# Hybrid decoder layer: small steps of the first two pairs moved, head norms over two tiles, and the softmax heads of the gate pair begun two groups later

## The chip, the cores and the metric

The kernel runs on one core of a Trainium2 chip. The metric is the device time of one execution in microseconds (us); the median of several runs is compared. The core's engines are named as in the profile: PE is TensorE (matmuls), PEld its weight loads, DVE is VectorE, ACT is ScalarE, POOL is GpSimd, and SP is SyncE, whose queue here issues nearly every transfer, one after the other.

## The reference

One decoder layer on 512 positions of width 2048, all in float32. Cut to what matters here:

```python
h = rms_norm(x, norm1_g)
proj = h @ w_in
qa, ka, va, ra, ga, qb, kb, vb = split(proj)
log_g = log_sigmoid(ga @ gla_gate_w2 + gla_gate_b) / 16
out_a = gla_mixer(qa, ka, va, ra, log_g, gla_onorm_g)    # ends in rms_norm(o) * silu(ra)
qb, kb = rms_norm(qb, q_norm_g), rms_norm(kb, k_norm_g)  # per head of 128
out_b = dilated_mixer(qb, kb, vb, rel_bias)              # causal softmax heads with a bias
x = x + concatenate([out_a, out_b]) @ w_out
h2 = rms_norm(x, norm2_g)
x = x + (silu(h2 @ w_gate) * (h2 @ w_up)) @ w_down
```

`qa` and `ka` are 512 columns wide, `va` and `ra` 1024 each, `ga` 16, and `qb`, `kb`, `vb` 1024 each. `gla_mixer` is a gated linear attention of 4 heads over chunks of 64 positions. `dilated_mixer` has 8 heads of 128 columns; the kernel computes it as one causal softmax whose bias depends on the distance alone.

## The kernel before

**Pairs.** All large products go through one scheme. A pair computes two blocks of 512 output columns for all 512 rows by seven half-sized products (Strassen's, in Winograd's form) in place of eight: `P1`, `P5`, `P6`, `P3`, `P7`, `P2`, `P4` in the later pairs. In the pairs around the change each product sums over four contraction groups, which makes 28 items of 12 matmuls with 128x512 outputs. The 12 are for precision: the operand is kept as a rounded part and a remainder, and so is the weight. Eight matmuls take the weight's rounded part `wh`, four its remainder `wl`. ScalarE makes `wh` (L373; L519 in the first pair), VectorE makes `wl` (L377; L527) and the differences of weight blocks that some products need (L298; L514). Such an item is called a group below, and in the prediction.

**Ends of products.** Accumulators are few (four banks, `acc`, and four more, `bank`, for everything else). Where a product ends whose value is needed again, ScalarE copies it to a `seed` tile (L324 with the row scale; L542 in the first pair, without), from a pool of six. A later product's end adds its own accumulator to that tile (`close`). Then `final` takes the finished block of 256 rows by 512 columns as two tiles: `final_proj` stores it (L1065) to device memory, from where the heads load it.

**The first pair** gives `qa` and `ka` and has its order written by hand, in the string `PLAN`. `h.k` makes `wh` of item k and `l.k` its `wl`; `mH.k` and `mL.k` are its matmuls; `sq`, `nA`, `nB`, `nC` build the row norm of `x` (squares, then on `xms` the mean, L691, Ln and Exp, L694 and L695, and a Newton step; the digit is the half of the rows); `gh` and `rank` belong to the 16 columns `ga`; `seedX`, `closeX` and `sclX` copy, close and scale block X. `scla` scales block `a`, a part of `qa`, by the norm of half 0 (L550), after which `final` stores it.

**The later pairs** are written by `stream`. After the eighth matmul of each group it calls `step()`, which counts down what was put off with `later(n, fn)` and then takes as many steps of the generators in `background` as the pair's `rate` says: `rate((84, 0.5))` is one step in two groups. The generators are the gates (`gates`), the bias tables (`bias_tables`, fed by a one-hot table), the four heads of linear attention (`gla_head`) and four couples of softmax heads (`dil_heads`, eight steps of two heads). The second step of a couple transposes and scales `q` and `k` (L954, L955). Each later one makes, for one block of 128 rows, the scores with Exp (L969), reciprocal and scaling (L973), then their transposition (L980, copied by L983) and the product with the values (L987, L999). With `hold` set, as in the gate pair, a weight difference is placed behind the last score emitted.

**Order.** SP's queue follows the code as emitted; a scheduler sets the order on PE, ACT and DVE from it. Names such as `oT`, `PT`, `v`, `kT` are single tiles that all background work uses in turn: a new user waits for the last.

**The pairs around the change.** Pair 2 gives `va` and runs `gates`, `bias_tables` and the first linear heads: four gate matmuls (L795, from `gas`, L789) give `ls_d` (L802), a head loads its part of it as `T` (L822), cumulates it on TensorE (L833), transposes `q` and `k` (L849), scales `q` into `qT` (L857) and forms its scores (L873). Pairs 3 and 5 give `qb` and `kb`, normalised per head in `heads_norm`; pair 4 gives `vb`; pair 6, the gate pair, gives `ra`. Its `final_gate` loads the finished linear attention `og` (L1103), multiplies it by `ra` (L1119), forms the sigmoid by Exp, Ln and Exp (L1120 to L1122), multiplies again (L1123), and two groups later transposes the result (L1078) into the operand of the product with `w_out`; pieces of that operand are split as `GATE` and `OUT` list them. In the gate pair the last two couples of softmax heads run, at a `rate` of their own.

## Time and profile before

| | us |
|---|---|
| median of 3 runs (1940.41 to 1941.84) | 1941.62 |
| the profiled execution | 1938.88 |
| its span, first to last instruction | 1937.1 |
| TensorE busy | 1918.9 |
| VectorE busy | 1650.3 |
| ScalarE busy | 1094.8 |
| GpSimd busy | 16.8 |

The profile is of one execution. A page gives busy times, groups of instructions and a chain of waits; from the trace behind it come the list of waits by engine, windows and timelines. A row of waits has the engine and tile that waited, the engine and tile that ended the wait, and total us, number and longest. A timeline row has start and duration in us, the engine (SPq is SP issuing a transfer), line, operation, tiles, and in brackets how long the engine stood idle before it and what ended that. A row of windows has the stretch, its length, and for each engine its busy time and its instructions; where it is limited to one line, that line's alone. Its last three figures are TensorE's granted clock as a share of full speed, the share of the transfer engines in use, and GB/s. Engines work side by side, so a busy time adds to the span only where another engine waits for it.

### The profile page before, as it was taken

What the parts mean: (1) busy time and instruction counts of PE and PEld (TensorE: products, weight loads), DVE (VectorE), ACT (ScalarE), POOL (GpSimd) and SP (SyncE); (2) the same over time, 40 slices, a digit from 0 to 9 for tenths busy, and PEclk for the clock granted to TensorE, in tenths of its full rate; (3) what the DMA queues carried; (4) which work ended last, traced back from release to release, by engine and by line L of the source; (5) the groups of instructions that cost most, each with busy time, mean ns of one, the idle gap of its engine ahead of it and who ended that gap; (6) DMA issues with size and microseconds to landing.
All of it is one profiled execution on the core that took longest, in us unless ns stands there. A gap on an engine that the chain in (4) does not pass through costs nothing.

```text
span 1937.1 us, 25614 instructions
## 1 busy us (share of the span) xinstructions
PE 1918.9 (99%) x9178; PEld 1662.9 (86%) x9178; DVE 1650.3 (85%) x1936; ACT 1094.8 (57%) x1634; POOL 16.8 (1%) x25
## 2 busy tenths in 40 slices
PE   9999999999999999999999999999999999999999
PEld 7888888888888888888888888888888888888887
DVE  8896887778799999878878878878879989989987
ACT  9564564667766675544544545544546646546443
POOL 1000100000000000000000000000000000000000
PEclk9999999999999999999999999999999999999999
DMA  8536555444536564455454454453555865855762
GB/s 337 195 109 220 168 180 173 140 157 146 185 131 208 177 213 130 136 180 161 137 180 156 138 185 142 152 185 122 172 169 175 292 210 184 297 190 180 244 218 66
DMA packets 150360, 345.75 MB, mean 178 GB/s; under 512 B 15494, under 2 KB 42671, under 8 KB 150232
## 3 DMA queue, kind: packets, MB, share of 16 engines
q1 hardware_dynamic: 149944, 343.98, 52.9%
q8 instruction: 72, 1.18, 0.3%
q14 instruction: 56, 0.46, 0.1%
q10 hardware_dynamic: 288, 0.14, 0.0%
HBM read 286.10 MB, written 60.31 MB: 179 GB/s over the span
## 4 chain that ended last, share of the span: by engine, by line
PE 87%; DVE 6%; DMA 4%; issue 2%; ACT 1%; SPq 0%; POOL 0%; DVEq 0%; ACTq 0%; POOLq 0%
PE acc L402 79%; DVE wl L377 2%; PE acc L474 2%; PE bank L1078 1%; PE bank L987 1%; PE bank L963 1%; DVE wa L298 1%; PE bank L980 0%; DVE AS L199 0%; DMA T<-in_xt 0%; DMA k<-in_gw 0%; PE bank L760 0%; DMA wb<-in_w_in 0%; PE bank L954 0%; PE bank L474 0%
## 5 line engine op out<-in xcount | busy, mean ns | idle before, releaser
L402 PE MATMUL acc<-wh,AS 128*128 128x512 f32 x3008 | 711.8, 379 | 0.0
L402 PEld LDWEIGHTS acc<-wh,AS 128*128 128x128 f32 x3008 | 568.2, 189 | 81.2 <-ACT wh L373 0.5
L373 ACT CAST wh<-wa 128x1024 fp32r<-128x1024 f32 x376 | 394.3, 1049 | 396.3 <-PE acc L402 367.6
L402 PE MATMUL acc<-wh,AA 128*128 128x512 f32 x2256 | 534.7, 380 | 0.5 <-ACT wh L373 0.5
L377 DVE TENSOR_TENSOR wl<-wa,wh 128x1024 fp32r<-128x1024 f32 x376 | 456.7, 1217 | 73.0 <-ACT wh L373 47.3
L402 PEld LDWEIGHTS acc<-wh,AA 128*128 128x128 f32 x2256 | 427.1, 189 | 61.7 <-ACT wh L373 0.9
L402 PE MATMUL acc<-wl,AS 128*128 128x512 f32 x1504 | 393.8, 384 | 1.8 <-DVE wl L377 1.6
L402 PEld LDWEIGHTS acc<-wl,AS 128*128 128x128 f32 x1504 | 280.0, 189 | 51.4 <-DVE wl L377 10.2
L402 PE MATMUL acc<-wl,AA 128*128 128x512 f32 x1128 | 296.4, 385 | 0.2
L402 PEld LDWEIGHTS acc<-wl,AA 128*128 128x128 f32 x1128 | 209.9, 189 | 31.4 <-DVE wl L377 2.4
L373 ACT CAST wh<-wb 128x1024 fp32r<-128x1024 f32 x94 | 98.6, 1049 | 123.6 <-PE acc L402 118.9
L373 ACT CAST wh<-wc 128x1024 fp32r<-128x1024 f32 x94 | 98.5, 1048 | 115.9 <-PE acc L402 107.8
L373 ACT CAST wh<-wd 128x1024 fp32r<-128x1024 f32 x94 | 98.6, 1049 | 102.2 <-PE acc L402 98.6
L377 DVE TENSOR_TENSOR wl<-wc,wh 128x1024 fp32r<-128x1024 f32 x94 | 114.5, 1219 | 40.4 <-ACT wh L373 40.4
L377 DVE TENSOR_TENSOR wl<-wd,wh 128x1024 fp32r<-128x1024 f32 x94 | 114.4, 1219 | 36.5 <-ACT wh L373 29.6
L298 DVE TENSOR_TENSOR wa<-wc,wa 128x1024 f32<-128x1024 f32 x94 | 114.4, 1219 | 32.9 <-DMA wc<-in_w_gate 22.1
L377 DVE TENSOR_TENSOR wl<-wb,wh 128x1024 fp32r<-128x1024 f32 x94 | 114.0, 1216 | 5.0 <-ACT wh L373 4.8
L298 DVE TENSOR_TENSOR wa<-wb,wa 128x1024 f32<-128x1024 f32 x94 | 113.6, 1218 | 1.2 <-DMA wb<-in_w_in 0.5
L298 DVE TENSOR_TENSOR wb<-wd,wb 128x1024 f32<-128x1024 f32 x94 | 114.0, 1216 | 0.4
L298 DVE TENSOR_TENSOR wa<-wd,wa 128x1024 f32<-128x1024 f32 x94 | 112.9, 1215 | 0.1
L340 DVE SCALAR_TENSOR_TENSOR seed<-acc,rs,seed 128x512 f32<-128x512 f32 x96 | 70.4, 745 | 29.4 <-PE acc L402 29.3
L324 ACT ACTIVATE seed<-acc,rs 128x512 f32<-128x512 f32 x96 | 60.6, 682 | 5.0 <-PE acc L402 4.9
(320 smaller groups left out, 1315.5 us busy)
## 6 DMA issues: line engine op xcount, KB each, us to landing
wa<-in_w_gate SPq DMA_DIRECT2D x44, 512.0 KB, 3.5
wb<-in_w_up SPq DMA_DIRECT2D x44, 512.0 KB, 4.3
wd<-in_w_up SPq DMA_DIRECT2D x44, 512.0 KB, 4.3
wc<-in_w_gate SPq DMA_DIRECT2D x44, 512.0 KB, 3.5
wa<-in_w_in SPq DMA_DIRECT2D x24, 512.0 KB, 4.6
wc<-in_w_in SPq DMA_DIRECT2D x24, 512.0 KB, 3.5
wb<-in_w_in SPq DMA_DIRECT2D x24, 512.0 KB, 5.4
wd<-in_w_in SPq DMA_DIRECT2D x24, 512.0 KB, 4.4
```

The costliest lines, as they stand in the source:

```text
L298: nc.vector.tensor_tensor(src, other, src, op=ALU.subtract)
L324: nc.scalar.activation(halves(t), unfolded(src[m]), AF.Copy, scale=self.scale(half, m))
L340: nc.vector.scalar_tensor_tensor(halves(seed[m]), unfolded(src[m]), self.scale(half, m), halves(seed[m]), op0=ALU.mult, op1=ALU.add,)
L373: nc.scalar.copy(high[k], sources[k])
L377: nc.vector.tensor_tensor(low[k], sources.pop(k), high[k].bitcast(F32), op=ALU.subtract)
L402: nc.tensor.matmul(p.dst[prod][m], a[:, jj, hl, m * P : (m + 1) * P], folded(w[i][:, jj, :]), start=fresh and g == 0 and i == 0 and jj == ...
L474: recent["pe"] = nc.tensor.matmul(dst[name][m], a[:, jj, hl, m * P : (m + 1) * P], folded(w[:, jj, :]), start=(name, m) not in opened, sto ...
L963: nc.tensor.matmul(lp[:, :n], qh[:, b * P : (b + 1) * P], kh[:, :n], start=True, stop=True)
L987: nc.tensor.matmul(op, vh[:, k, :], lgs[b][:, k * P : (k + 1) * P], start=(k == 0), stop=(k == b))
L1078: nc.tensor.transpose(bk[:, jj, m * P : (m + 1) * P], tiles[m][:, f : f + P], ident)
```

## The change

Five edits of order and of small steps; no matmul is added or removed.

1. In `PLAN` the norm of row half 0 (`nA.0`, `nB.0`, `nC.0`) and the scaling of block `a` (`scla.0`, `scla.1`) move ahead, the scaling from behind `h.24` to right behind `h.19`; `gh.1` moves one item back.
2. `gates` gets a yield ahead of the copy of the gate columns and another ahead of its four matmuls, so these come later; the first part of the one-hot table in `bias_tables` uses tile `PT` in place of `v`.
3. `heads_norm` takes both tiles of a block at once: eight squares, then one chain of mean, Ln, Exp and Newton step over eight columns in place of two over four; the stores follow both. The small tile `rt` doubles for it.
4. `final_gate` has its `og` loaded two groups into the product that closes the block, by `ahead`, a hook that `begin` already had with three groups; it was loaded at the close.
5. The gate pair's `rate` holds the background back for four groups in place of three and for two in place of one, and then takes 0.93 steps a group in place of 0.9.

```diff
--- before.py
+++ after.py
@@ -71,29 +71,29 @@
 
 
 PLAN = """
...
-mL.18 mH.19 +W.20 nA.1 h.20 lo.S2.3 mL.19 lo.S3.3 h.21 mH.20 l.20 nB.1 l.21 mL.20 h.22 +S4.3
-mH.21 nC.1 l.22 mL.21 h.23 nA.0 mH.22 nB.0 l.23 nC.0 mL.22 h.24 mH.23 scla.0 l.24 scla.1 mL.23
...
+seedc.1 lo.S4.1 mL.14 hi.S4.2 l.15 h.16 mH.15 lo.S4.2 seedc.0 l.16 mL.15 nA.0 lo.A22.1 mH.16
+lo.A22.2 hi.S3.2 +W.17 mL.16 +W.19 h.17 nB.0 rank.1 lo.S3.0 lo.S3.2 hi.S3.1 +W.22 l.17 mH.17 +W.18
+D.d.3 D.b.3 lo.S3.1 nC.0 h.18 mL.17 +W.21 h.19 scla.0 scla.1 mH.18 l.18 hi.S3.3 l.19 mL.18 mH.19
...
 """
 
 
@@ -174,7 +174,7 @@
     ident, tri, stri, causal = (mats[:, i, :] for i in range(4))
 
     def rsqrt_mean(sq, n):
-        y = work("rt", (P, 4), bufs=4)[:, : sq.shape[-1]]
+        y = work("rt", (P, 8), bufs=4)[:, : sq.shape[-1]]
         nc.vector.tensor_scalar(sq, sq, 1.0 / n, EPS, op0=ALU.mult, op1=ALU.add)
         nc.scalar.activation(y, sq, AF.Ln)
         nc.scalar.activation(y, y, AF.Exp, scale=-0.5)
@@ -311,7 +311,7 @@
                 self.dst["P2"] = self.accs()
             ahead = getattr(self.final, "ahead", None)
             if ahead and prod in CLOSES:
-                later(3, lambda: ahead(*CLOSES[prod]))
+                later(getattr(self.final, "units", 3), lambda: ahead(*CLOSES[prod]))
 
         def seeds(self, src, half):
             res = []
@@ -657,7 +657,7 @@
         rel = work("T", (33, 8))
         nc.gpsimd.memset(rel[32:33, :], 1.0)
         load(rel[0:32, :], ins["rel_bias"])
-        for c0, cn, t0, t1 in ((0, 512, "v", "qT"), (512, NB - 512, "oT", "kT")):
+        for c0, cn, t0, t1 in ((0, 512, "PT", "qT"), (512, NB - 512, "oT", "kT")):
             oh = work(t0, (33, cn))
             load(oh, ins["onehot"][:, c0 : c0 + cn])
             bp = bank()
@@ -770,6 +770,7 @@
                          ap=[[0, 8], [512, 16], [1, 512]]))
         gbias = work("oT")
         load(gbias, bass.AP(tensor=ins["gla_gate_b"].tensor, offset=0, ap=[[0, P], [1, 512]]))
+        yield
         ga = work("k", (32, 512))
         nc.scalar.copy(ga, rank["p"][:32, :])
         ga4 = work("kT")
@@ -789,6 +790,7 @@
             nc.vector.tensor_tensor(
                 gas[r, :], ga4[r, :], gas[r, :].bitcast(F32), op=ALU.subtract
             )
+        yield
         yield
         for t in range(4):
             zp = bank()
@@ -1029,17 +1031,22 @@
             yield from g
 
 
-    def heads_norm(t):
-
-        ss = work("ss", (P, 4), bufs=4)
+    def heads_norm(tiles):
+
+        ss = work("ss", (P, 8), bufs=4)
         jk = work("jk", (P, P // 2)).bitcast(mybir.dt.bfloat16)
-        tv = t.rearrange("p (h d) -> p h d", h=4)
-        for h in range(4):
-            nc.scalar.activation(jk, tv[:, h, :], AF.Square, accum_out=ss[:, h : h + 1])
+        by_head = [t.rearrange("p (h d) -> p h d", h=4) for t in tiles]
+        for m in range(2):
+            for h in range(4):
+                nc.scalar.activation(
+                    jk, by_head[m][:, h, :], AF.Square, accum_out=ss[:, 4 * m + h : 4 * m + h + 1]
+                )
         rsqrt_mean(ss, P)
-        nc.vector.tensor_tensor(
-            tv, tv, ss.unsqueeze(2).to_broadcast([P, 4, P]), op=ALU.mult
-        )
+        for m in range(2):
+            nc.vector.tensor_tensor(
+                by_head[m], by_head[m],
+                ss[:, 4 * m : 4 * m + 4].unsqueeze(2).to_broadcast([P, 4, P]), op=ALU.mult,
+            )
 
     ready = {
         "va0": lambda: [gla_head(0), gla_head(1)],
@@ -1058,10 +1065,10 @@
                 tiles = emitted(acc_, lambda m: row_scale(half, m))
             name = (n1, n2)[which]
             dst = proj[name]
+            if name[:2] in ("qb", "kb"):
+                heads_norm(tiles)
             for m in range(2):
                 r = half * 256 + m * P
-                if name[:2] in ("qb", "kb"):
-                    heads_norm(tiles[m])
                 store(dst[r : r + P, :], tiles[m])
             if half == 1 and name in ready:
                 background.extend(ready[name]())
@@ -1095,13 +1102,16 @@
             store(dsts[b][half], d)
             done.add((id(dsts[b]), half))
 
+    normed = {}
+
+    def gate_ahead(half, which):
+        both = apool.tile([P, 2, 512], F32, name=nm("og"), tag="A")
+        for m in range(2):
+            load(both[:, m, :], ong_d[2 * half + m][:, which * 512 : (which + 1) * 512])
+        normed[half, which] = [both[:, m, :] for m in range(2)]
+
     def final_gate(half, which, tiles, acc_):
-        og = []
-        spare = apool.tile([P, 2, 512], F32, name=nm("og"), tag="A")
-        for m in range(2):
-            t = spare[:, m, :]
-            load(t, ong_d[2 * half + m][:, which * 512 : (which + 1) * 512])
-            og.append(t)
+        og = normed.pop((half, which))
         if tiles is None:
             tiles = [cpool.tile([P, 512], F32, name=nm("cr"), tag="C") for _ in range(2)]
             src = acc_
@@ -1133,6 +1143,8 @@
 
         later(2, turn)
 
+    final_gate.ahead, final_gate.units = gate_ahead, 2
+
     def part(src, half):
         def get(t=None):
             assert (id(src), half) in done
@@ -1235,7 +1247,7 @@
     pair(opx, rows_in, col(3072), col(4096), final_proj("qb0", "kb0"), flow, row_scale)
     pair(opx, rows_in, col(5632), col(5120), final_proj("vb1", "vb0"), flow, row_scale)
     pair(opx, rows_in, col(3584), col(4608), final_proj("qb1", "kb1"), flow, row_scale)
-    pair(opx, rows_in, col(2048), col(2560), final_gate, scripted(rate((3, 0), (1, 1), (1, 0), (1, 1), (1, 0.9)), GATE), row_scale, hold=True)
+    pair(opx, rows_in, col(2048), col(2560), final_gate, scripted(rate((4, 0), (1, 1), (2, 0), (1, 1), (1, 0.93)), GATE), row_scale, hold=True)
 
 
     rows_mix = [(1024 + 256 * g, 256 * order[g]) for g in range(4)]
```

The scheduler turns this into the following orders. A row gives the line, the operation, the tiles written and read, and the size; numbers in names count tiles.

ScalarE, at the end of the first pair, before: Ln and Exp of a row norm (L694, L695; the second such couple is half 0's), the casts of `wh` (L519), the scaling of block `a` (L550), and the next seeds (L542).

```order
L519 CAST wh_909<-wa_244 128x1024
L694 ACTIVATE rs_105<-xms 128x2
L695 ACTIVATE rs_105<-rs_105 128x2
L519 CAST wh_929<-wa_246 128x1024
L519 CAST wh_949<-wb_860 128x1024
L694 ACTIVATE rs_105<-xms 128x2
L695 ACTIVATE rs_105<-rs_105 128x2
L519 CAST wh_972<-wd_858 128x1024
L550 ACTIVATE seed_520<-seed_520,rs_102 128x512
L550 ACTIVATE seed_525<-seed_525,rs_102 128x512
L542 COPY seed_992<-acc_412 128x512
L542 COPY seed_994<-acc_413 128x512
```

The same place after the change, from the norm of half 0 to that of half 1 (L208 is an operand cast):

```order
L694 ACTIVATE rs_105<-xms 128x2
L695 ACTIVATE rs_105<-rs_105 128x2
L208 CAST AS_125_848<-xT_108 128x2x256
L519 CAST wh_870<-wb_264 128x1024
L519 CAST wh_877<-wb_271 128x1024
L550 ACTIVATE seed_520<-seed_520,rs_102 128x512
L550 ACTIVATE seed_525<-seed_525,rs_102 128x512
L208 CAST AS_132_893<-xT_114 128x2x256
L519 CAST wh_912<-wa_240 128x1024
L519 CAST wh_920<-wa_244 128x1024
L694 ACTIVATE rs_105<-xms 128x2
L695 ACTIVATE rs_105<-rs_105 128x2
```

The norm of half 0 stood behind six casts of `wh` that it now stands ahead of; the two scalings, which stood right ahead of the seeds, now have five casts of `wh` behind them before the seeds come.

TensorE, the first head of linear attention in pair 2, before: the last matmuls of pair 2 (L402), then the head's cumulation (L833, L834), transpositions (L849, `mats` holds the identity) and scores (L873), with nothing between.

```order
L402 MATMUL acc_1062<-wl_1679,AA_47_338 128x512
L402 MATMUL acc_1063<-wl_1679,AA_47_338 128x512
L833 MATMUL bank_1598<-mats,T_1553 128x128 x3
L834 MATMUL bank_1599<-T_1553,mats 128x512
L849 MATMUL bank_1652<-mats,q_1558 128x128 x4
L849 MATMUL bank_1653<-mats,k_1560 128x128 x4
L873 MATMUL bank_1691<-qT_1662,kT_1666 64x128
L873 MATMUL bank_1691<-L_1605,kT_1666 64x128
L873 MATMUL bank_1691<-qT_1662,kT_1666 64x128
```

The same head after the change (lines are two further on: L851 is the transposition, L875 the score):

```order
L851 MATMUL bank_1652<-mats,q_1558 128x128 x4
L851 MATMUL bank_1653<-mats,k_1560 128x128 x4
L402 MATMUL acc_1062<-wl_1621,AA_89_595 128x512
L402 MATMUL acc_1063<-wl_1621,AA_89_595 128x512
L402 MATMUL acc_1062<-wl_1621,AA_89_595 128x512
L402 MATMUL acc_1063<-wl_1621,AA_89_595 128x512
L402 MATMUL acc_1062<-wh_1636,AA_85_572 128x512 x2
L402 MATMUL acc_1063<-wh_1636,AA_85_572 128x512 x2
L402 MATMUL acc_1062<-wh_1636,AA_85_572 128x512 x2
L402 MATMUL acc_1063<-wh_1636,AA_85_572 128x512 x2
L875 MATMUL bank_1691<-qT_1662,kT_1666 64x128
L875 MATMUL bank_1691<-L_1605,kT_1666 64x128
```

Twelve matmuls now lie between the transpositions and the first score (eight rows, of which four stand for two matmuls each); the cumulation stands a group and a half further ahead, outside these rows.

ScalarE in the gate pair, where the second of its couples of softmax heads begins, before: scalings of `q` and `k` (L955), the first Exp of scores (L969), the six activations of the first gate close (L1120 to L1122).

```order
L955 ACTIVATE qT_4748<-bank_4788,gq 128x512
L955 ACTIVATE kT_4749<-bank_4794,gk 128x512
L198 CAST AA_941_4959<-top_4857 128x2x256
L373 CAST wh_4843<-wb_4346 128x1024
L969 ACTIVATE L_4824,mx_4825<-L_4824,mx_4825 128x128
L969 ACTIVATE PT_4833,mx_4834<-PT_4833,mx_4834 128x128
L373 CAST wh_4864<-wb_4383 128x1024
L373 CAST wh_4917<-wb_4404 128x1024
L983 COPY L_4824<-bank_4891 128x128
L983 COPY PT_4833<-bank_4902 128x128
L1120 ACTIVATE seed_4702<-seed_4702 128x512
L1120 ACTIVATE seed_4738<-seed_4738 128x512
```

The same after the change (L957, L971, and L1130 to L1132 for the close):

```order
L957 ACTIVATE qT_4720<-bank_4758,gq 128x512
L957 ACTIVATE kT_4721<-bank_4764,gk 128x512
L1130 ACTIVATE seed_4576<-seed_4576 128x512
L1130 ACTIVATE seed_4630<-seed_4630 128x512
L1131 ACTIVATE seed_4576<-seed_4576 128x512
L1131 ACTIVATE seed_4630<-seed_4630 128x512
L1132 ACTIVATE seed_4576<-seed_4576 128x512
L1132 ACTIVATE seed_4630<-seed_4630 128x512
L971 ACTIVATE L_4807,mx_4808<-L_4807,mx_4808 128x128
L971 ACTIVATE PT_4816,mx_4817<-PT_4816,mx_4817 128x128
L373 CAST wh_4826<-wb_4332 128x1024
L985 COPY L_4807<-bank_4840 128x128
```

The first Exp of this couple, ahead of the close with four other rows between, now stands right behind the close's six activations.

SP's queue at the same place, before: loads of weights (L259), the loads of `og` for the second close (L1103), inputs of the next pair (L1254), and the heads' results (L1003).

```order
L259 DMA wc_5078<-in_w_in 128x1024
L259 DMA wa_5239<-in_w_out 128x1024
L259 DMA wa_5257<-in_w_out 128x1024
L259 DMA wa_5294<-in_w_out 128x1024
L259 DMA wa_5331<-in_w_out 128x1024
L1103 DMA og_5091<-ong_d_134 128x512
L1103 DMA og_5091<-ong_d_135 128x512
L1254 DMA q_5689<-in_x 128x512
L1254 DMA k_5692<-in_x 128x512
L259 DMA wb_5349<-in_w_out 128x1024
L1003 DMA mix_d_143<-oT_4821 128x2x256
L1003 DMA mix_d_143<-r_4830 128x2x256
```

And after, where L1110 is the load of `og`:

```order
L1153 DMA top_4770<-mix_d_142 128x512 x2
L1110 DMA og_4801<-ong_d_134 128x512
L1110 DMA og_4801<-ong_d_135 128x512
L259 DMA wa_5170<-in_w_out 128x1024
L259 DMA wa_5188<-in_w_out 128x1024
L259 DMA wa_5225<-in_w_out 128x1024
L259 DMA wa_5259<-in_w_out 128x1024
L1110 DMA og_5010<-ong_d_132 128x512
L1110 DMA og_5010<-ong_d_133 128x512
L1266 DMA q_5617<-in_x 128x512
L1266 DMA k_5620<-in_x 128x512
L259 DMA wb_5277<-in_w_out 128x1024
```

The load for the second close (`ong_d_134`, `ong_d_135`) stood behind four loads of `wa` and now stands ahead of them, and that for the third (`ong_d_132`, `ong_d_133`) has come into its old place. The one for the first close lies ahead of these rows, between the last stores of `qb` and the heads' loads of it.

More of the change, by code (lines that the diff above doesn't have):

```diff
@@ L97 @@
++W.20 nA.1 h.20 lo.S2.3 mL.19 lo.S3.3 h.21 mH.20 l.20 nB.1 l.21 mL.20 h.22 +S4.3 mH.21 nC.1 l.22
+mL.21 h.23 mH.22 l.23 mL.22 h.24 mH.23 l.24 mL.23 seedd.0 seedd.1 closed.0 mH2.23 closed.1 scld.0
+scld.1 mL2.23 h.25 mH.24 hi.S4.3 l.25 lo.S4.3 mL.24 mH2.24 closec.0 closec.1 sclc.0 sclc.1 mL2.24
+closeb.1 sclb.1 closeb.0 sclb.0
 """
```

37 lines of the change are left out of this document (16 added, 21 removed).

## Prediction

> **What bounds the kernel now.** I read the page first, for who is busy, then the waits of TensorE, then the timeline around each wait.
>
> ```profile
> PE 1918.9 (99%) x9178; PEld 1662.9 (86%) x9178; DVE 1650.3 (85%) x1936; ACT 1094.8 (57%) x1634; POOL 16.8 (1%) x25
> 231.47 10.36 PE acc L402 x48
> ...
> PE bank L1078 <- DVE seed L1123: 2.0, 2, 1.8
> PE acc L474 <- ACT seed L542: 2.0, 1, 2.0
> PE acc L402 <- DVE wl L377: 1.6, 5, 0.6
> PE bank L873 <- DVE qT L857: 1.5, 1, 1.5
> ...
> PE bank L954 <- DMA q<-qb: 0.9, 1, 0.9
> ...
> PE bank L795 <- DVE gas L789: 0.6, 1, 0.6
> ...
> PE bank L664 <- DMA v<-in_onehot: 0.4, 1, 0.4
> ...
> PE bank L980 <- DVE L L973: 0.3, 1, 0.3
> ```
>
> TensorE is busy 99% of the span, and its matmuls run at a steady 10.36 / 48 = 0.216 us (second row, from the chain of waits). The change leaves their number alone. So it can only win what TensorE waits, and the list of waits is short: the columns are total, times, longest. The change touches six of these rows: L1078, L474, L873, L954, L795 and L664, 7.4 us together. That is the ceiling for the waits themselves; one of them has a sequel on the clock, below.
>
> **The first pair's scaling (L474).** The rows are from the timeline.
>
> ```profile
> 74.03 2.01 ACT L519 CAST wh<-wa 128x1024 fp32r<-128x1024 f32 x2 [2.63 <-DVE xms L691]
> ...
> 83.33 1.34 ACT L550 ACTIVATE seed<-seed,rs 128x512 f32<-128x512 f32 x2
> 84.07 0.94 SPq L1065 DMA_DIRECT2D qa<-seed  x2
> 84.77 1.03 PE L474 MATMUL acc<-wl,AA 128*128 128x512 f32 x4
> 87.17 1.22 ACT L542 COPY seed<-acc 128x512 f32<-128x512 f32 x2 [2.51 <-DMA qa<-seed]
> 87.81 2.19 PE L474 MATMUL acc<-wh,AA 128*128 128x512 f32 x8 [2.02 <-ACT seed L542]
> ```
>
> The scaled tiles `seed` of block `a` are stored at 84.07; their buffers are wanted by the copies at 87.17, which wait for those stores, and TensorE waits for the copies, which free its accumulator. In the new order the two scalings stand five weight casts earlier, at about 71, right ahead of the row at 74.03, where ScalarE stood idle for 2.63 us: 1.34 us fit in. The stores then go out some 12 us sooner and the copies run at 84.7, ahead of the end of the matmuls of 84.77 at 85.8. Both stores pass SP ahead of one weight load of the next pair, which is wanted 20 us later. **Gain 2.0 us**, and nothing in exchange.
>
> **Gates and first GLA head (L795, L664, L873).** The two added yields put the four gate matmuls about 1.6 to 2 groups of 12 matmuls later, over 4 us, against a wait of 0.6; the one-hot factor moves to a tile that is free long before, against 0.4. Gain 1.0 us. What was one lump is now spread out:
>
> ```profile
> 155.04 1.39 SPq L822 DMA_DIRECT2D T<-ls_d  x3
> DMA to landing us min/median/max: 3.7/3.7/3.7
> 174.59 0.60 PE L849 MATMUL bank<-mats,q 128*128 128x128 f32 x4
> ...
> 176.56 0.42 DVE L857 TENSOR_TENSOR qT<-L,decay 128x256 f32<-128x256 f32 x1
> ...
> 177.12 0.29 PE L873 MATMUL bank<-qT,kT 128*64 128x128 f32 x1 [1.50 <-DVE qT L857]
> ```
>
> The chain from the first transposition to the product `qT` takes 176.98 - 174.59 = 2.4 us. In the lump TensorE has only 1.0 us of transpositions for it. Now 12 matmuls lie between, 2.6 us more, so the 1.5 us are covered with 1.1 us to spare. Could the first piece come too early? It needs the fourth `ls_d` tile. That load follows the same four `va` stores on SP as the three at 155.04; shifted by the 3 us won so far it goes out at 152 and lands, 3.7 us later, at 155.7, against a need at about 159. **Gain 1.5 us**, bounds 0.5 (VectorE busy with one weight remainder of 1.2 us just then, of which 0.1 to 1.0 shows) and 1.5.
>
> **Norms over two tiles, heads two groups later (L954).**
>
> ```profile
> 260.00:470.00 210.00, 209.07 (x1059) 182.24 (x1058) 168.85 (x283) 131.23 (x313) 2.29 (x3) 1.00 0.50 163
> 461.19 0.68 DVE L1040 TENSOR_TENSOR cout<-cout,ss 128x512 f32<-128x512 f32 x1
> ...
> 463.95 0.37 SPq L943 DMA_DIRECT2D q<-qb  x1
> ...
> 466.91 0.66 PE L954 MATMUL bank<-mats,q 128*128 128x128 f32 x4 [0.93 <-DMA q<-qb]
> ```
>
> The merged norm saves 32 VectorE and 16 ScalarE instructions of some 0.15 to 0.2 us. The window row (PE, weight loads, VectorE, ScalarE) shows TensorE idle for 0.9 of 210 us there, with VectorE 41 us free: worth nothing but at its end, where the last norm, store and load of `q` run into TensorE. The transpositions move from 0.1 to 1.7 groups into that stretch, 4.1 us. Against it the two `og` loads stand ahead of `q` on SP, 0.9 us of issue and a shared transfer, and the first tile's store now waits for the joint norm. The wait cannot be under 0, and at worst stays: **gain 0.8 us**, between 0 and 0.9.
>
> **The gate pair's factor (L1078).**
>
> ```profile
> 542.18 0.90 SPq L1103 DMA_DIRECT2D og<-ong_d  x2
> ...
> 545.36 1.21 DVE L377 TENSOR_TENSOR wl<-wa,wh 128x1024 fp32r<-128x1024 f32 x1
> 548.73 1.36 DVE L1119 TENSOR_TENSOR og<-seed,og 128x512 f32<-128x512 f32 x2 [2.16 <-DMA og<-ong_d]
> ...
> 553.10 0.33 PE L1078 MATMUL bank<-mats,seed 128*128 128x128 f32 x1 [1.77 <-DVE seed L1123]
> ...
> 556.02 2.94 PE L402 MATMUL acc<-wh,AA 128*128 128x512 f32 x8
> 555.00:559.00 4.00, 4.00 (x12) 3.19 (x12) 4.00 (x6) 1.73 (x5) 0.00 (x0) 0.61 0.30 112
> ```
>
> The load of `og` is issued with the close and lands 6.5 us later, between weight loads; VectorE stands idle 2.16 us for it and TensorE 2.0. Right behind that, the granted clock is 0.61 for 4 us (last row, the figure after the engines' columns): 4 x 0.39 = 1.6 us lost. With the load two groups into the product it is there before the close. Recovered: 2.0 + 1.6 = 3.6 us.
>
> [...]
>
> **What the two groups cost.** The second couple of heads now starts its scores one group closer to the first gate close, and on ScalarE their exponentials stand behind the close's six activations. Rows for the new chain, the nearest there are:
>
> ```profile
> 474.02 0.40 ACT L969 ACTIVATE L<-L,mx 128x128 f32<-128x128 f32 x1
> ...
> 475.73 0.29 DVE L973 TENSOR_SCALAR L<-L,mx 128x128 f32<-128x128 f32 x1
> ...
> 502.48 0.60 PE L954 MATMUL bank<-mats,q 128*128 128x128 f32 x4
> ...
> 503.63 0.68 ACT L955 ACTIVATE q<-bank,gq 128x512 f32<-128x512 f32 x1
> ...
> 505.35 0.70 ACT L955 ACTIVATE kT<-bank,gk 128x512 f32<-128x512 f32 x1
> ...
> 531.04 1.15 ACT L1120 ACTIVATE seed<-seed 128x512 f32<-128x512 f32 x2
> ...
> 533.14 1.14 ACT L1122 ACTIVATE seed<-seed 128x512 f32<-128x512 f32 x2
> ```
>
> From the first transposition: 1.15 to the first scaling (502.48 to 503.63), 2.4 for four scalings (to 506.05), 3.2 for the six activations (531.04 to 534.28), 0.9 for two exponentials and 0.5 for reciprocal and scaling: 8.2 us. TensorE meanwhile has the transpositions (1.7), 24 matmuls (5.2) and the first scores (0.4), 7.3: a **new wait of 0.9 us**. In the old order two groups lay between scores and turn, and there was none. Two places more: the fourth score block's scaling now stands behind a weight remainder and an operand remainder, 1.2 + 0.7, so 0 to 1.9; and the close of the third product has its second tile two remainders and two passes behind its first, 3.8 us, where TensorE has 1.1 us of matmuls between, so 0 to 2.7. VectorE had 3.2 us free in 505 to 555 and is ahead by the 2.16 us it no longer idles, which speaks for the lower halves; I take 0.8 each. New waits 2.5, net of the factor **1.1 us**.
>
> **The sum.** 2.0 + 1.0 + 1.5 + 0.8 + 1.1 = 6.4 us. The profiled execution took 1938.9 (span 1937.1 and 1.8 around it), so 1932.5 for it. The median of the runs is 1941.6, 2.7 above that execution, so I predict **1935.2 us**; with the bounds of the terms 1933 to 1938.
>
> **Rivals.** *All of it comes*: no new wait forms, gain 2.0 + 1.0 + 1.5 + 0.9 + 3.6 = 9.0, 1932.6. For it: VectorE is 2.16 us ahead. Against: the 8.2 against 7.3 above. *The gate pair gives its part back and more*: new waits at their upper ends, 0.9 + 1.9 + 2.7 = 5.5, and another spell of low clock, 1.6; net -3.5 there, total 1.8, 1939.8, no change. [...] *Slower: VectorE becomes the bound in the gate pair.* It has no room there:
>
> ```profile
> 506.00:530.00 24.00, 3.75 (x16) 1.00 0.52 181
> 506.00:530.00 24.00, 2.88 (x8) 1.00 0.52 181
> ```
>
> These are its score and scaling instructions of one couple of heads, 6.6 us, now pushed into the closes. If all of it shows, with two low spells (3.2) and none of the 3.6 recovered, the total is 5.3 - 9.8 = -4.5, 1946.1. It decides once the heads' chain falls a whole group behind TensorE; against it, two pairs of weight differences that stood there before now stand ahead of the closes, which gives back 2.4 us.
>
> **How the numbers follow.** The forecast gets 0.5, all of it 0.15, clock spell 0.12, given back 0.17, slower 0.06. About 0.2%, 3.9 us, is what a measurement of this kernel can tell from no change: faster is below 1937.7. To it go nearly all of the forecast, all of the second, two thirds of the third: 0.72. Same takes most of given back and the rests, 0.23, slower 0.05. The range, 1931 to 1940, takes in all but the slower case and the tails.
>
> **What would show it.** Right: no wait of L474 on `seed`, none of L873 on `qT`, no idle of VectorE for `og`, L1078's wait under 0.5. New: a wait of the heads' transpositions on the scaled `L` some 35 us before the old place of L1078, and on the last close. Wrong: waits in the gate pair above 4 us together, a clock below 1.00 there, or a wait of the first GLA head on the `ls_d` loads.

## The result, and the profile after

| | before | changed |
|---|---|---|
| median of 6 runs, us | 1941.88 | 1934.3 |
| lowest to highest | 1940.41 to 1944.06 | 1931.72 to 1938.05 |
| profiled execution | 1938.88 | 1935.39 |
| its span | 1937.1 | 1933.6 |
| VectorE, ScalarE busy | 1650.3, 1094.8 | 1646.6, 1093.8 |

The ratio is 0.9965 (0.9954 to 0.9975), some 6.8 us. The predicted 1935.2 is 0.9 us off. The waits of TensorE in the changed kernel, with total, number and longest in us:

```profile
PE acc L474 <- ACT wh L519: 4.1, 3, 2.8
PE acc L402 <- DVE wl L377: 1.5, 4, 0.8
PE bank L638 <- POOL L L635: 1.3, 1, 1.3
PE bank L1085 <- DVE seed L1133: 1.1, 1, 1.1
PE bank L664 <- DMA oT<-in_onehot: 0.7, 1, 0.7
PE bank L982 <- DVE L L975: 0.6, 1, 0.6
PE acc L402 <- ACT wh L373: 0.5, 1, 0.5
PE acc L474 <- DVE wl L527: 0.2, 1, 0.2
```

Gone are the waits of L474 on `seed`, of L873 on `qT`, of L795, and of L954 on `q`. The third close (now L1085) fell from 2.0 to 1.1. The wait for the one-hot table did not go: it is 0.7 now, on `oT`. And the row on top, which no step of the prediction has, grew from 1.2 us (at most 0.5 at once) to 4.1 for casts in the first pair, 2.8 of them at once. Its place in the timeline (start, duration, engine, and in brackets the idle time before it):

```profile
30.19 7.17 POOL L724 COPY v<-k 128x128 f32<-128x128 f32 x1 [28.64 <-DMA k<-in_gw]
38.12 0.35 ACT L737 CAST gs<-v 128x192 fp32r<-128x192 f32 x1 [3.74 <-POOL v L726]
39.47 2.99 PE L474 MATMUL acc<-wh,AS 128*128 128x512 f32 x8 [2.85 <-ACT wh L519]
```

GpSimd's copy took 7.17 us; in the profile before it took 1.34. ScalarE waits for it with a cast of the gate columns, the next `wh` stands behind that cast, and TensorE waits for `wh`. The experiments have to say whether the change did that.

To see where time goes, the table takes the same matmul of the main products in each profiled execution (the 200th, 320th and so on, at the time that it has before) and gives how much more a stretch took than before. Where two kernels order the small matmuls differently, only points with equally many of them behind are used. The names are those of the experiments in the next section.

| stretch before, us | 0 to 57 | to 90 | to 137 | to 180 | to 463 | to 546 | to 596 | to the end |
|---|---|---|---|---|---|---|---|---|
| what lies there | start | first scaling | gates, one-hot | first GLA head | norms | `q`, heads | third close | no edit |
| changed | +2.7 | -1.7 | -0.2 | -1.6 | 0.0 | -0.9 | -3.1 | +1.2 |
| changed, again | -0.3 | -2.1 | -0.3 | -1.6 | 0.0 | -1.0 | -3.4 | +0.9 |
| `p1_order` | -0.2 | -2.1 | -0.3 | 0.0 | 0.0 | -0.1 | +0.5 | +1.2 |
| `p2_gates` | -0.4 | +0.1 | -0.2 | -1.6 | +0.1 | 0.0 | -0.8 | +0.5 |
| `tile` | +1.2 | +0.6 | +0.6 | -1.6 | +0.1 | +0.2 | -0.9 | +0.4 |
| `p3_norms` | -0.3 | -0.3 | -0.3 | 0.0 | +0.4 | +0.3 | -0.8 | +1.0 |
| `p4_gatepair` | +2.2 | +1.7 | -0.3 | 0.0 | +0.3 | -1.2 | -3.5 | +1.4 |
| `og_only` | +0.5 | +1.4 | +0.2 | 0.0 | 0.0 | +2.8 | -1.7 | +2.0 |
| `pace_only` | +0.3 | +1.4 | -0.4 | 0.0 | 0.0 | +4.6 | -1.6 | +0.7 |

The last stretch holds no edit, and there every other execution took 0.4 to 2.2 us longer than the profile before. That execution was a short one, as its 1938.88 against a median of 1941.88 says. Not every figure is an edit's work. Some are spells in which TensorE's granted clock was 0.50: the profile before has one of 3.41 us between 546 and 596; `tile`, `p4_gatepair`, `og_only` and `pace_only` have one near 89 us, behind the unchanged wait for the seeds of 2.0 to 2.4 us (the mean clock of the 6 us behind it was 0.72 or 0.73), which is most of their +0.6 to +1.7 there; `og_only` and `pace_only` have one more between 463 and 546 (a mean of 0.72 and 0.55 over 6 us), of about 3.4 us and of 6 to 7 us, worked out from these means and from those of `pace_only` over 480 to 520 us, 0.98, and 520 to 560 us, 0.94.

### The profile page after: what moved, and what is told of

Read it like the earlier page. It is cut to its first block, busy times and chain, and to the rows that moved or that the text cites. A ratio compares the mean times of both kernels' runs of the same rounds, so it can differ in the third digit from the quotient of the medians.

```text
span 1933.6 us, 25568 instructions
## 1 busy us (share of the span) xinstructions
PE 1918.9 (99%) x9178; PEld 1662.7 (86%) x9178; DVE 1646.6 (85%) x1904; ACT 1093.8 (57%) x1618; POOL 22.3 (1%) x25
## 4 chain that ended last, share of the span: by engine, by line
PE 85%; DVE 7%; DMA 4%; issue 3%; ACT 1%; POOL 0%; SPq 0%; DVEq 0%; ACTq 0%; POOLq 0%
PE acc L402 78%; DVE wl L377 2%; PE bank L1085 1%; DVE wa L298 1%; PE bank L989 1%; PE bank L965 1%; PE acc L474 1%; DMA mix_d<-r 1%; PE bank L982 0%; DVE AS L199 0%; DMA wc<-in_w_gate 0%; DMA T<-in_xt 0%; PE bank L474 0%; DMA wb<-in_w_in 0%; DMA k<-in_gw 0%
## 5 line engine op out<-in xcount | busy, mean ns | idle before, releaser
L402 PE MATMUL acc<-wh,AS 128*128 128x512 f32 x3008 | 711.0, 379 | 0.0
L402 PEld LDWEIGHTS acc<-wh,AS 128*128 128x128 f32 x3008 | 568.4, 189 | 81.1 <-ACT wh L373 0.3
L402 PE MATMUL acc<-wh,AA 128*128 128x512 f32 x2256 | 533.5, 379 | 0.5 <-ACT wh L373 0.5
L402 PEld LDWEIGHTS acc<-wh,AA 128*128 128x128 f32 x2256 | 426.1, 189 | 61.3 <-ACT wh L373 0.9
L402 PE MATMUL acc<-wl,AS 128*128 128x512 f32 x1504 | 393.9, 384 | 1.8 <-DVE wl L377 1.5
L402 PEld LDWEIGHTS acc<-wl,AS 128*128 128x128 f32 x1504 | 279.6, 189 | 52.4 <-DVE wl L377 10.6
L402 PE MATMUL acc<-wl,AA 128*128 128x512 f32 x1128 | 296.8, 385 | 0.4
L402 PEld LDWEIGHTS acc<-wl,AA 128*128 128x128 f32 x1128 | 209.6, 189 | 33.1 <-DVE wl L377 3.3
```

The lines of the kernel that those rows point to most:

```text
L402: nc.tensor.matmul(p.dst[prod][m], a[:, jj, hl, m * P : (m + 1) * P], folded(w[i][:, jj, :]), start=fresh and g == 0 and i == 0 and jj == ...
```

## The experiments

Every kernel was timed in five rounds beside the kernel before. The first seven take the change apart.

**The order of the first pair alone** (edit 1 of the change).

```diff
-mL.18 mH.19 +W.20 nA.1 h.20 ... h.23 nA.0 mH.22 nB.0 l.23 nC.0 mL.22 h.24 mH.23 scla.0 l.24 scla.1
+... seedc.0 l.16 mL.15 nA.0 lo.A22.1 ... h.17 nB.0 ... nC.0 h.18 ... h.19 scla.0 scla.1 mH.18
```

> The kernel before with the first edit alone (the order of the first pair). Theory: the wait of 2.0 us of the matmuls of L474 on the copies L542 goes, and some 0.8 us of it comes back ahead of it, where the Newton steps of the norm now stand ahead of two remainders; net 1.2 to 1.7 us faster, all of it between 70 and 90 us. GpSimd's first copy (L724), 1.34 us before and 7.17 us in the changed kernel's profile, is chance: as likely short as long. Rival: moving the copy of the gate columns makes it long; then it is 7 us here, and TensorE loses 2.7 us at 36 us, in all slower by about 1 us.

Ratio 0.9987 (0.9978 to 0.9996). The timeline at the seeds:

```profile
83.56 1.07 ACT L542 COPY seed<-acc 128x512 f32<-128x512 f32 x2
...
85.86 1.89 PE L474 MATMUL acc<-wh,AA 128*128 128x512 f32 x8
```

Neither row has a wait in brackets any more, where 2.51 and 2.02 us stood before. The stretch is 2.1 us shorter, more than the 1.2 to 1.7 expected: of the 0.8 us expected back, 0.4 came, between 70 and 73 us, and a wait of 0.3 right behind the seeds went too. GpSimd's copy took 1.06 us here, so moving the gate columns does not by itself make it long, as the rival had it.

**The gates and the one-hot tile alone** (edit 2), and **the tile without the yields.**

```diff
-        for c0, cn, t0, t1 in ((0, 512, "v", "qT"), (512, NB - 512, "oT", "kT")):
+        for c0, cn, t0, t1 in ((0, 512, "PT", "qT"), (512, NB - 512, "oT", "kT")):
```

> The kernel before with the second edit alone (two more yields in the gates, the one-hot tile). Theory: the 1.5 us of L873 on qT go, the 0.6 of L795 go, and the wait for the one-hot table stays or grows to 0.7 to 0.9, now on tile oT, which the fourth gate releases late: 1.5 to 2.0 us faster. Rival, the prediction's term: the wait for the table goes as well, 2.5 us. GpSimd's first copy, if chance, may be long here too, and costs 2.7 us then.

> The kernel before with the one-hot tile alone (PT in place of v, no added yields). Theory: the wait of 0.4 us for the first part goes, but the second part in oT still waits for the gates' last reader, which without the yields comes earlier: at most 0.4 us faster, and the 1.5 us of L873 stay. Rival: the tile, not the yields, is what spreads the first head; then L873 waits under 0.3 us and it is 1.5 us faster or more.

`p2_gates`: 0.9985 (0.9976 to 0.9993). `tile`: 0.9996 (0.9987 to 1.0004), an interval that holds both zero and the 1.6 us that its trace shows; so the trace has to speak. The timeline of `tile`, at the gates and at the first linear head:

```profile
110.41 0.47 PE L795 MATMUL bank<-w2s,gas 128*128 128x512 f32 x1 [0.60 <-DVE gas L789]
...
171.38 0.60 PE L849 MATMUL bank<-mats,k 128*128 128x128 f32 x4
171.73 1.11 PE L402 MATMUL acc<-wl,AA 128*128 128x512 f32 x4
172.68 1.89 PE L402 MATMUL acc<-wh,AA 128*128 128x512 f32 x8
174.50 0.32 PE L873 MATMUL bank<-qT,kT 128*64 128x128 f32 x1
```

Twelve matmuls stand between the transpositions and the scores although no yield was added, and L873 waits for nothing. So the rival of the last expectation holds: the tile spreads the first head, and both kernels gain the same 1.6 us by it. How the tile does that was not followed to its end; an early trace of it is that SP issues the head's first loads of `T` at 131.67 us in place of 136.98. The 0.6 us at L795 stay, as they must without the yields. With the yields they go, and this comes for it in `p2_gates`:

```profile
133.41 0.38 PE L664 MATMUL bank<-oT,T 33*8 33x128 f32 x2 [0.67 <-DMA oT<-in_onehot]
```

The later gates hold `oT`, their bias, longer, and the second part of the table wants the same tile. The yields give 0.6 and take 0.7: together nothing.

**The norms alone** (edit 3).

```diff
-                if name[:2] in ("qb", "kb"):
-                    heads_norm(tiles[m])
+            if name[:2] in ("qb", "kb"):
+                heads_norm(tiles)
```

> The kernel before with the third edit alone (head norms over two tiles). Theory: 46 instructions fewer on engines with time to spare; TensorE's wait of 0.9 us for q at 467 us stays within 0.5 of it either way, so within 0.5 us of before. Rival: the shorter norm is what removes that wait, and the wait is gone here: 0.9 us faster.

Ratio 1.0004 (0.9996 to 1.0013): nothing. The pages count 48 instructions fewer, 32 on VectorE and 16 on ScalarE. The wait for `q` is still in the list:

```profile
PE bank L954 <- DMA q<-qb: 1.1, 1, 1.1
```

**The gate pair alone** (edits 4 and 5), **the early load without the pace** and **the pace without the early load.**

```diff
-            load(t, ong_d[2 * half + m][:, which * 512 : (which + 1) * 512])
+    final_gate.ahead, final_gate.units = gate_ahead, 2
-rate((3, 0), (1, 1), (1, 0), (1, 1), (1, 0.9))
+rate((4, 0), (1, 1), (2, 0), (1, 1), (1, 0.93))
```

> The kernel before with the fourth and fifth edit (the factor loaded ahead, heads begun two groups later). Theory: the wait for q (0.9) goes, the waits of L1078 fall from 2.5 us to 1.1 or 1.3 with no half clock behind, new waits of 0.3 to 0.5 in the heads: 3.0 to 4.0 us faster, about half of the whole change. Rival: without the merged norm VectorE comes late in the pair and the half clock returns: 1 to 2 us faster.

> The kernel before with the factor og loaded ahead, and the old pace. Theory: most of the gate pair's gain is the load: VectorE no longer idles 2.2 us for og, the waits of L1078 fall from 2.5 us to under 1.3, while the wait for q at 467 us stays or grows to 1.0 to 1.9, because two loads stand ahead of it: 0.5 to 2.5 us faster, all at the third close. Rival: the pace is what matters, the waits of L1078 stay above 1.5 us, and the kernel is no faster.

> The kernel before with the new pace alone, og loaded at the close as before. Theory: the wait of 0.9 us for q goes, new waits of 0.3 to 0.5 us in the heads, the waits of L1078 stay at 2.0 to 2.5 us with or without a half clock by chance: within 1 us of before. Rival: heads that come later relieve VectorE at the third close too, L1078 waits under 1.3 us, 2 to 3 us faster.

Both together: 0.9976 (0.9967 to 0.9985), 4.7 us, more than the 3.0 to 4.0 expected and the largest part of the change. The load alone: 0.9999 (0.9991 to 1.0008). The pace alone: 1.0005 (0.9995 to 1.0014). Two halves of nothing make the largest gain, and the traces show why. The profiles of the two halves are each the slowest of eleven executions (1944.16 and 1943.85 against medians of 1939.75 and 1941.46), so it is their waits that count here and not their totals. `og_only`, where the heads begin at the old time:

```profile
465.30 0.32 SPq L1103 DMA_DIRECT2D og<-ong_d  x1
466.05 0.37 SPq L943 DMA_DIRECT2D q<-qb  x1
466.47 0.50 SPq L943 DMA_DIRECT2D qT<-qb  x1
467.02 0.49 SPq L1103 DMA_DIRECT2D og<-ong_d  x1
470.66 0.66 PE L954 MATMUL bank<-mats,q 128*128 128x128 f32 x4 [1.93 <-DMA q<-qb]
```

The first `og` transfer goes ahead of `q`, and the wait for `q` doubles from 0.9 to 1.9, with half clock behind it (the granted clock was 0.72 in the mean from 470.66 to 476.66). `pace_only`, where `og` is loaded at the close (L1119 multiplies with it, L1120 begins the sigmoid, L969 is the Exp of the scores):

```profile
508.24 0.90 SPq L1103 DMA_DIRECT2D og<-ong_d  x2
...
511.78 0.69 DVE L1202 TENSOR_TENSOR top<-top 128x512 f32<-128x512 f32 x1 [3.39 <-DMA top<-mix_d]
513.72 0.69 DVE L1119 TENSOR_TENSOR og<-seed,og 128x512 f32<-128x512 f32 x1 [1.25 <-DMA og<-ong_d]
514.44 0.63 ACT L1120 ACTIVATE seed<-seed 128x512 f32<-128x512 f32 x1 [2.76 <-DVE og L1119]
...
517.63 0.39 ACT L969 ACTIVATE L<-L,mx 128x128 f32<-128x128 f32 x1
...
519.44 0.45 PE L980 MATMUL bank<-mats,L 128*128 128x128 f32 x1 [2.93 <-DVE mx L972]
```

The heads now stand behind the first steps of the close on VectorE and ScalarE. The close waits for `og`, 513.72 - 508.24 = 5.5 us after its issue, and on VectorE it stands behind a tile `top` that comes late as well; the heads wait for the close, and TensorE 2.93 us for the heads. With both edits, in `p4_gatepair`, that wait is 0.5 and the one for `q` is gone. The pace moves `q` clear of the early load; the early load keeps the close from holding up the moved heads. Each pays what the other one costs. The two halves alone do not do what their theories say: `og_only` waits at L1078 for 1.2 us at the third close and 0.6 at the fourth, above the 1.5 of its rival, and gains nothing, as the rival had it; `pace_only` stays within its 1 us though its new wait is 2.9 and not 0.3 to 0.5, because L1078 fell to 1.1, as its rival had it.

**Is GpSimd's long copy of the change's making?** The changed kernel again; the copies of the gate columns some 5 us later on ScalarE; and one more copy on GpSimd at the start.

```diff
-+S1.1 ... mL.7 gh.1 h.9 ... hi.S1.2 gh.0 hi.A22.2 ... lo.S2.0 hi.A22.1
++S1.1 ... mL.7 h.9 ... hi.S1.2 hi.A22.2 ... lo.S2.0 gh.1 gh.0 hi.A22.1
```

```diff
+    first = work("v", (P, 128))
+    nc.gpsimd.tensor_copy(first, idle[:, :128])
     warm = bank()
```

> The changed kernel once more, unaltered, beside the next two. Theory: 1933 to 1935 us, 5 to 7 us below before; GpSimd's first copy is short or long by chance, and the profile shows TensorE waiting 2 to 3 us at 36 us only where it is over 4 us. Rival: TensorE waits there whatever the copy's length.

> The changed kernel with both copies of the gate columns (gh.1, gh.0) moved some 10 us later, to behind lo.S2.0. Theory: GpSimd's first copy takes 1 to 7 us by chance, and the 2.7 us that TensorE lost at 36 us in the changed kernel's profile is that; here TensorE doesn't wait at 36 us whether the copy is short or long, the median is 0.5 to 1.5 us below the changed kernel's (0.996 to 0.9955 of before) and the spread is narrower than its 6 us. Rival: the loss at 36 us has another cause and stays, ratio 0.9965 as for the changed kernel.

> The changed kernel with one more small copy on GpSimd at its start, 28 us ahead of L724, of a tile that is not used further. Theory: what varies is the first copy of an execution; here the added copy takes what L724 took, L724 takes under 1.5 us, TensorE waits under 0.6 us at 36 us, and the spread is that of gh_late, some 4 us. Rival: L724 is slowed by the traffic of its time; then it is as likely long as before, and the spread stays at 6 us.

Again: 1931.19, 0.996 (0.9947 to 0.9973). `gh_late`: 1932.48, 0.996 (0.9948 to 0.9973). `pool_warm`: 1931.96, 0.9966 (0.9955 to 0.9978). The timeline and the waits of the changed kernel's second profile:

```profile
30.77 0.71 POOL L724 COPY v<-k 128x128 f32<-128x128 f32 x1 [29.22 <-DMA k<-in_gw]
```

```profile
PE bank L1085 <- DVE seed L1133: 0.9, 1, 0.9
...
PE bank L664 <- DMA oT<-in_onehot: 0.6, 1, 0.6
...
PE bank L982 <- DVE L L975: 0.5, 1, 0.5
...
PE acc L474 <- ACT wh L519: 0.2, 1, 0.2
```

The same kernel, with a copy of 0.71 us, has 0.2 us in place of the 4.1 for the casts, and 4.2 us less span (1929.4 against 1933.6), 3.0 of them in the first 57 us. Over the 14 profiles of this case L724 took 0.29 to 1.44 us in ten, and 5.03, 7.17, 7.35 and 12.06 in four, among them `p4_gatepair`, which has the first pair of before. So the change is not needed for a long copy. Whether it makes one likelier stays open: three of the seven profiles with the new order of the first pair have one, and one of the seven with the old order.

Beside the copy's end stands a row of VectorE. First the changed kernel's profile, then its second one, then `gh_turn`, the next experiment, where the copy ran from 30.27 for 12.06 us, then the profile before and `p4_gatepair`, where it ran from 30.39 for 1.34 us and from 30.29 for 5.03:

```profile
36.53 0.68 DVE L211 TENSOR_TENSOR AS<-xT,AS 128x512 fp32r<-128x512 f32 x1
39.97 0.69 DVE L211 TENSOR_TENSOR AS<-kT,AS 128x512 fp32r<-128x512 f32 x1 [2.76 <-ACT AS L208]
```

```profile
30.10 1.22 DVE L527 TENSOR_TENSOR wl<-wc,wh 128x1024 fp32r<-128x1024 f32 x1
32.06 1.23 DVE L514 TENSOR_TENSOR wa<-wb,wa 128x1024 f32<-128x1024 f32 x1 [0.74 <-DMA wb<-in_w_in]
```

```profile
40.97 1.22 DVE L527 TENSOR_TENSOR wl<-wa,wh 128x1024 fp32r<-128x1024 f32 x1
```

```profile
30.36 1.22 DVE L527 TENSOR_TENSOR wl<-wc,wh 128x1024 fp32r<-128x1024 f32 x1
31.65 1.23 DVE L514 TENSOR_TENSOR wa<-wb,wa 128x1024 f32<-128x1024 f32 x1
```

```profile
33.94 1.22 DVE L527 TENSOR_TENSOR wl<-wa,wh 128x1024 fp32r<-128x1024 f32 x1
37.39 0.69 DVE L504 TENSOR_TENSOR kT<-kT,PT 128x512 f32<-128x512 f32 x1 [2.23 <-ACT kT L494]
```

In the changed kernel's profile VectorE works without a pause from the copy's start until 36.53 + 0.68 = 37.21, and the copy ends at 37.36. In the second one VectorE stands still from 31.32, for a weight that lands late, and the copy ends at 31.48. In `gh_turn` the row shown ends at 42.19 and the copy at 42.33; in the profile before it is 31.58 and 31.73, and VectorE's next instruction starts at 31.65; in `p4_gatepair` VectorE works without a pause from the copy's start until 35.16, and the copy ends at 35.32. So in these five profiles the copy ended 0.14 to 0.16 us behind the end of a VectorE instruction, and in the changed kernel's profile and `p4_gatepair`, with copies of 7.17 and 5.03 us, VectorE had no pause until then. That the one sets the other is my reading, and not shown: no run moved VectorE's work to test it. In the changed kernel's profile VectorE's pause behind 37.21 was one of 2.76 us for a tile from ScalarE, which stood idle for 3.74 us until the copies of the gate columns were done.

`gh_late`'s own copy was short, 0.64 us, and the spread of its runs, 1930.6 to 1934.4, told little. `pool_warm` gives no support to its theory of a slow first copy: L724 (L726 there) took 1.43 us with another copy ahead of it, as long as the longer of the ten short ones, TensorE waited 0.9 us at 37 us, and the runs reach from 1930.4 to 1939.2, more than the theory allows.

**The transposition of the third close a group later**, with the later copies of `gh_late`.

```diff
-        later(2, turn)
+        later(3 if (half, which) == (0, 0) else 2, turn)
```

> The changed kernel with both copies of the gate columns later, as in gh_late, and the transposition of the third close one group later. Theory: the wait left at L1085 (1.1 us in the changed kernel, 0.7 in gh_late) goes, for a group of 12 matmuls gives 2.6 us more; the pieces of the next operand that need its result are wanted four groups later: 0.7 to 1.1 us faster than gh_late. Rival: VectorE is full there, and the wait moves to the next operand's pieces: no faster than gh_late, ratio 0.996.

Ratio 0.9965 (0.9953 to 0.9977), no faster than `gh_late`. The timeline, at the start and at the closes:

```profile
30.27 12.06 POOL L724 COPY v<-k 128x128 f32<-128x128 f32 x1 [28.73 <-DMA k<-in_gw]
...
43.10 0.60 ACT L737 CAST gs<-v 128x192 fp32r<-128x192 f32 x2 [4.71 <-POOL v L726]
...
46.26 3.78 PE L474 MATMUL acc<-wh,AS 128*128 128x512 f32 x8 [2.89 <-ACT wh L519]
...
561.81 0.88 PE L1085 MATMUL bank<-mats,cr 128*128 128x128 f32 x6 [1.00 <-DVE cr L1133]
```

The wait of the third close is gone, and one of 1.00 us stands at the fourth (tile `cr`): the rival, with the wait moved to the next close instead of the operand's pieces. And against a copy of 12 us the later place does not hold either.

**The second part of the one-hot table in another tile**, on the changed kernel.

```diff
-(512, NB - 512, "oT", "kT")
+(512, NB - 512, "k", "kT")
```

> The changed kernel with the second part of the one-hot table in tile k in place of oT. Theory: its load waits for the fourth gate's last reader of oT, so TensorE's wait of 0.7 us for it goes: 0.7 to 0.9 us faster than the changed kernel in the trace (0.9961 of before). Rival: the load waits for SP's queue, not for the tile, and the wait of 0.7 us stays.

Ratio 0.9968 (0.9957 to 0.9979), as the changed kernel. The wait of 0.7 us is gone, so the tile was its cause. But:

```profile
130.60 0.73 SPq L669 DMA_DIRECT2D rep_d<-bias_d  x1
...
145.05 1.87 SPq L259 DMA_DIRECT2D wc<-in_w_in  x4
...
156.20 1.13 PE L402 MATMUL acc<-wl,AA 128*128 128x512 f32 x4 [1.38 <-DVE wl L377]
```

The bias tables ended sooner, and with that the order of SP's queue changed: four loads of `wc` go out together at 145.05, where in the changed kernel's profile three of them went out at 131.41, 134.33 and 138.38. A weight comes late, and TensorE waits 1.38 us for its remainder. The part on the kernel says that SP's queue follows the code as emitted; that is not so. Both profiles of the changed kernel have one and the same order of 935 transfers, while `onehot_k`, with nothing but the tile exchanged, has another: the scheduler orders SP's queue too.

## Why the prediction was right, and where not

The time was right, 1935.2 for 1934.3, and of the five cases the forecast is nearest. Its terms were not all right, and that errors cancel is luck. The stretches with edits add up to -7.5 and -8.4 in the two profiles of the changed kernel, where -6.4 was forecast; the ratio gives 6.8 (4.9 to 8.9). The gates were 0.7 too high, the gate pair 2.1 to 2.5 too low. Of the signs named, the waits of L474 on `seed` and of L873 and VectorE's idle for `og` are gone, and a wait on the scaled `L` has come; the third close did not fall below 0.5.

- *First pair, 2.0*: 1.7 and 2.1 in the two profiles of the changed kernel, 2.1 alone. The mechanism is the one forecast. "Nothing in exchange" was too much: with the norm's steps on VectorE now ahead, TensorE comes 0.4 later between 70 and 73 us, 0.8 in the first of the two profiles.
- *Gates and one-hot, 1.0*: 0.2 to 0.3. The failing step is "the one-hot factor moves to a tile that is free long before, against 0.4". That holds for the first of two parts; the second stayed on `oT`, which the later gates hold. I read the row of L664 as one tile.
- *First GLA head, 1.5*: 1.6, but by another cause. "The two added yields" are not needed to spread the head; the tile does it, as `tile` shows. Whether the yields would do it without the tile was not run. The size came from a row of the trace and held. The cause came from the diff, and was never priced apart.
- *Norms, 0 of their own*: 0.
- *`q` two groups later, 0.8*: the wait of 0.9 is gone, as forecast.
- *The gate pair*: the mis-sized terms. From 463 to 596 us the prediction has -0.8, -3.6 and +2.5, together -1.9; the two profiles have -4.0 and -4.4. The chain of 8.2 us came as summed, as the changed kernel's timeline shows:

```profile
505.72 0.60 PE L956 MATMUL bank<-mats,q 128*128 128x128 f32 x4
...
513.90 0.30 PE L982 MATMUL bank<-mats,L 128*128 128x128 f32 x1 [0.63 <-DVE L L975]
```

From 505.72 to 513.90 it is 8.2 us, and 8.0 in the second profile. TensorE had 7.5 us of work for it instead of 7.3, so the wait is 0.6 and 0.5 (0.9 expected). The term that failed is the fourth block's scaling: no wait came there (0.8). The third close waits 1.1 and 0.9 (0.8). New waits are thus 1.8 and 1.4 in place of 2.5. Two small waits of before, 0.3 at L980 and 0.2 for `wl`, went as well, which no term has. Of the rest, some 0.6 us stand in no wait that the profiles list, and their cause stays open.
- *The clock, 1.6 of the 3.6 recovered*: real against that one execution, but too high, and not a fixed price. `p2_gates`, `tile` and `p3_norms` have the same close, with waits of 1.7 to 1.9 us and no half clock, and took only 0.8 to 0.9 us less than before from 546 to 596. First `p2_gates`, timeline and window (granted clock third from the end), then the window of `p1_order` 2 us behind its wait of 2.24:

```profile
551.09 0.33 PE L1080 MATMUL bank<-mats,seed 128*128 128x128 f32 x1 [1.79 <-DVE seed L1125]
```

```profile
553.00:557.00 4.00, 4.00 (x20) 3.52 (x19) 4.00 (x6) 2.82 (x6) 0.00 (x0) 1.00 0.31 111
```

```profile
552.50:555.50 3.00, 3.00 (x9) 2.37 (x8) 3.00 (x4) 1.97 (x4) 0.00 (x0) 0.50 0.45 156
```

A wait of 1.77 us before had half clock behind it, one of 1.79 in `p2_gates` had not. Over all profiles: of 30 waits from 0.9 to 1.5 us none was followed by half clock, of 14 from 1.7 to 2.4 seven were, and of four from 2.85 to 2.93 all. The profile before has one of each kind near 2 us: the wait of 1.77, with a spell, and the one of 2.02 for the seeds, which ends at 87.81, with none (a clock of 1.00 from 87.81 to 93.81). Its spell starts at 554.715 and lasts 3.413 us, and one more starts behind the last matmuls, at 1937.113: 405 times 3.4133 us later. In the changed kernel's profile the two start at 40.325 and 1934.722, 555 times 3.4133 us apart. Cut into stretches of that length, counted from 554.715, the profile before looks like this at the wait of 2.02 (first two rows) and at that of 1.77 (last two):

```profile
83.68:87.09 3.41, 2.12 (x10) 1.51 (x8) 1.00 (x1) 0.99 (x2) 0.00 (x0) 1.00 0.99 320
87.09:90.50 3.41, 2.69 (x12) 2.11 (x13) 1.32 (x2) 2.98 (x5) 0.00 (x0) 1.00 0.43 163
551.30:554.72 3.42, 1.37 (x10) 1.16 (x10) 3.42 (x6) 3.42 (x6) 0.00 (x0) 1.00 0.62 207
554.72:558.13 3.41, 3.41 (x9) 2.70 (x8) 3.41 (x4) 2.01 (x4) 0.00 (x0) 0.50 0.44 163
```

The wait of 2.02 lies in two stretches, with 3.41 - 2.12 = 1.29 and 3.41 - 2.69 = 0.72 us of idle, and the clock stays. The one of 1.77, with a second of 0.27 behind it, lies in one, TensorE is idle for 3.42 - 1.37 = 2.05 us of it, and the next has half clock. In the changed kernel's profile the stretch from 36.91 to 40.33 has 2.56 us of idle, most of its wait of 2.85, and the spell follows it. The other stretches of these two profiles, from 5 to 1925 us, have at most 1.28 us of idle, and no spell follows them. For the other profiles the stretches are not shown. With half of the 14 waits near 2 us followed by a spell, the fair price of that term was about half of 0.8 to 0.9, some 0.4, an estimate from the seven of 14.
- *The rest*: 1.2 us came back behind 596, and 2.7 were lost to GpSimd at the start. The first is no edit's, and for the second no tie to the change is shown. Against the medians they drop out by the way the sum was carried over: 2.7 were added for a profile that was that much below its median.

Of the rivals, "slower: VectorE becomes the bound" can be seen in one profile, when one half of the gate pair's edit is left out: `pace_only` loses 3.0 us from 463 to 596, with 6 to 7 us of half clock in them, and its heads stand behind the close as that rival had it. Its median is no slower than before. With both halves even that does not come.

## What to carry to other kernels

Price an edit in pairs where one instruction stands in the way of another's gain: here an early load and a later start were each worth nothing, and 4.7 us together. When a shared tile is renamed or released sooner, follow every user of every tile of that step, and the order of the load queue behind it. And where a profile is one execution, ask of each spell in it, a slow clock or a late copy, whether the next execution will have it too, before it goes into the sum at full price.

## What the runs showed of the hardware

- A copy of 128x128 on GpSimd, behind 28 to 31 us of idling, took 0.29 to 1.44 us in ten profiles and 5.03 to 12.06 in four. In the five whose rows stand above it ended 0.14 to 0.16 us behind the end of a VectorE instruction. In the changed kernel's profile and `p4_gatepair`, with copies of 7.17 and 5.03 us, the first 57 us were 2.7 and 2.2 us longer than before; in the other seven of the table they were between 0.4 us shorter and 1.2 us longer. The share of the transfer engines from 30 to 37 us was 1.03 both in the profile before, with a copy of 1.34 us, and in the changed kernel's. Whether an edit that gives VectorE a pause makes the copy short is not shown.
- TensorE's granted clock was 0.50 for 3.41 us behind the wait of 1.77 us in the profile before and behind that of 2.85 us in the changed kernel's; in these two the stretch of 3.41 us ahead of the spell had 2.05 and 2.56 us of idle. In `gh_turn` and `pace_only` it was 0.50 for 6 to 7 us, at waits of 2.89 and 2.93 us. As single waits, none of the 30 of 0.9 to 1.5 us in the 14 profiles had such a spell behind it, seven of the 14 of 1.7 to 2.4 us had, and all four of 2.85 to 2.93 us.
